# Row softmax on one core: row maximum added, buffers in one ring in place, per-row division, fixed program order, no guard instructions

## The chip, the core and the metric

The kernel runs on one core of one Trainium2 chip. The metric is device time in microseconds, the median of several executions. The span in a profile is about 2 us shorter than that time (161.6 us against 163.6 us before), because it covers the instructions of the program alone.

## The reference

```python
def setup_inputs():
    batch, seq, dim = 16, 1024, 512
    return {"x": np.random.randn(batch, seq, dim).astype(np.float32)}

def reference(x):
    x_max = np.max(x, axis=-1, keepdims=True)
    exp_x = np.exp(x - x_max)
    return (exp_x / np.sum(exp_x, axis=-1, keepdims=True)).astype(np.float32)
```

There are 16384 rows of 512 fp32 numbers: 33.55 MB in and 33.55 MB out.

## The kernel before

The rows are taken in 16 chunks of 128 partitions x 8 rows x 512, 2 MB each. A load goes out from the SP queue. ScalarE (ACT) makes eight exponentials per chunk, one for each row of a partition, and sums them on the way. VectorE (DVE) makes reciprocals of the eight sums and multiplies the whole chunk once by a broadcast. The store goes out from the ACT queue. The row maximum is switched off by an option: these inputs do not overflow without it. POOL's copies and memsets ("guard") compute nothing that is used.

```python
    x_pool = ctx.enter_context(tc.tile_pool(name="xp", bufs=XBUFS))      # 7
    e_pool = ctx.enter_context(tc.tile_pool(name="ep", bufs=EBUFS))      # 4
    ...
    use_max = os.environ.get("SM_USEMAX", "0") == "1"
    ...
    for t in range(nchunks):
        x_tile = x_pool.tile([P, R, d], mybir.dt.float32)
        nc.sync.dma_start(out=x_tile, in_=x_t[t])
        nc.gpsimd.tensor_copy(out=guard_tile, in_=x_tile[:, 0, 0:1])
        if use_max:
            ...  # reduce_max of the chunk to neg_max [P, R]
        e_tile = e_pool.tile([P, R, d], mybir.dt.float32)
        ...
        for r in range(R):
            nc.scalar.activation(
                out=e_tile[:, r, :], in_=x_tile[:, r, :],
                func=mybir.ActivationFunctionType.Exp,
                bias=neg_max[:, r : r + 1] if use_max else 0.0,
                scale=1.0, accum_out=sums[:, r : r + 1],
            )
        ...
        nc.vector.reciprocal(out=recip, in_=sums)
        recip_b = recip.unsqueeze(2).to_broadcast([P, R, d])
        nc.vector.tensor_mul(out=e_tile, in0=e_tile, in1=recip_b)
        nc.scalar.dma_start(out=out_t[t], in_=e_tile)
    for b in range(min(EBUFS, nchunks)):
        e_tile = e_tiles[nchunks - 1 - b]
        nc.gpsimd.memset(e_tile[:, 0, 0:1], 0.0)
```

Here a scheduler chooses the order of instructions on each engine. It gives ACT sixteen exponentials and then two stores, for most pairs of chunks.

The softmax here doesn't subtract the row's maximum and nothing guards it: scores larger than these inputs give would overflow.

## Time and profile before

| | before |
|---|---|
| time | 163.57 us (163.49 to 163.68, 3 runs) |
| span in the profile | 161.6 us |
| DVE / ACT busy | 74.0 us (46%) / 80.8 us (50%) |
| moved by DMA | 67.13 MB, 33.55 read and 33.55 written |

From the page of the kernel before: the span, each engine's busy time, and the row of 40 equal slices. A digit is the busy share of a slice in tenths; the last row is what the DMA engines moved in each slice.

```profile
span 161.6 us, 456 instructions
DVE 74.0 (46%) x32; ACT 80.8 (50%) x257; POOL 18.5 (11%) x24
DVE  0006970994196419082000008941992499069600
ACT  3089519924893481900000199339906970995000
DMA  5999999999999999999999999999999999999993
GB/s 150 434 434 426 434 373 422 432 430 430 438 426 426 446 422 426 450 422 426 446 410 442 438 418 438 434 422 440 426 430 442 418 434 442 418 434 442 418 434 146
```

The DMA row reads 9 from the second slice to the last but one, at about 430 GB/s, while DVE and ACT both have slices of 0. 67.13 MB at 430 GB/s are 156 us (worked out). The start and the end make up the rest. The Trainium skill, "Perfetto Trace Analysis", section What "DMA-bound" means, lists the 16 DMA engines themselves as one thing that such a kernel can be bound on. That is the case here: the DMA row stays at 9 where DVE and ACT fall to 0. What inside the engines or behind them sets the 430 GB/s, the trace does not show.

From the page's groups: line, engine, operation, shapes, count, then total busy us and mean ns of one, then the idle time before it and what ended it.

```profile
L61 ACT ACTIVATE e_tile<-x_tile 128x512 f32<-128x512 f32 x128 | 78.5, 615 | 66.1 <-DMA x_tile<-in_x_dram 35.1
L74 DVE TENSOR_TENSOR e_tile<-e_tile,recip 128x4096 f32<-128x4096 f32 x16 | 70.8, 4425 | 0.5
L49 POOL COPY guard_tile<-x_tile 128x1 f32<-128x1 f32 x16 | 17.9, 1116 | 119.0 <-DMA x_tile<-in_x_dram 119.0
```

From the page, the chain of waits by engine, as shares of the span:

```profile
DMA 52%; ACT 28%; DVE 17%; issue 1%; ACTq 1%; POOLq 0%; SPq 0%
```

The end of the same chain in order of time: start us, length us, what.

```profile
152.35 8.28 DMA out_dram<-e_tile
160.62 0.02 issue
160.65 0.04 POOLq L80
...
160.75 0.11 POOLq L106
```

The last store is issued at 152.35 us and has landed at 160.62 us. The last four stores land 4.8 us apart (POOL's four memsets, which wait for them, start at 146.22, 151.07, 155.92 and 160.75 us), and that is the time of one 2 MB transfer at the full rate. So the DMA engines never ran dry, even with a last store as late as this. The chain names ACT with 28%, but the DMA row is full during those stretches, so ACT time was not paid for there.

### The profile page before, as it was taken

What the parts mean: (1) busy time and instruction counts of PE and PEld (TensorE: products, weight loads), DVE (VectorE), ACT (ScalarE), POOL (GpSimd) and SP (SyncE); (2) the same over time, 40 slices, a digit from 0 to 9 for tenths busy, and PEclk for the clock granted to TensorE, in tenths of its full rate; (3) what the DMA queues carried; (4) which work ended last, traced back from release to release, by engine and by line L of the source; (5) the groups of instructions that cost most, each with busy time, mean ns of one, the idle gap of its engine ahead of it and who ended that gap; (6) DMA issues with size and microseconds to landing.
All of it is one profiled execution on the core that took longest, in us unless ns stands there. A gap on an engine that the chain in (4) does not pass through costs nothing.

```text
span 161.6 us, 456 instructions
## 1 busy us (share of the span) xinstructions
DVE 74.0 (46%) x32; ACT 80.8 (50%) x257; POOL 18.5 (11%) x24
## 2 busy tenths in 40 slices
DVE  0006970994196419082000008941992499069600
ACT  3089519924893481900000199339906970995000
POOL 0000000034090001000000006200082000000000
DMA  5999999999999999999999999999999999999993
GB/s 150 434 434 426 434 373 422 432 430 430 438 426 426 446 422 426 450 422 426 446 410 442 438 418 438 434 422 440 426 430 442 418 434 442 418 434 442 418 434 146
DMA packets 4610, 67.13 MB, mean 415 GB/s; under 512 B 512, under 2 KB 512, under 8 KB 512
## 3 DMA queue, kind: packets, MB, share of 16 engines
q1 hardware_dynamic: 2304, 33.56, 49.4%
q10 hardware_dynamic: 2304, 33.56, 48.5%
q14 instruction: 2, 0.02, 0.0%
HBM read 33.55 MB, written 33.55 MB: 415 GB/s over the span
## 4 chain that ended last, share of the span: by engine, by line
DMA 52%; ACT 28%; DVE 17%; issue 1%; ACTq 1%; POOLq 0%; SPq 0%
DMA x_tile<-in_x_dram 35%; ACT e_tile L61 28%; DMA out_dram<-e_tile 17%; DVE e_tile L74 16%; DVE recip L71 1%; ACTq L76 1%; POOLq L106 0%; POOLq L80 0%; SPq L47 0%
## 5 line engine op out<-in xcount | busy, mean ns | idle before, releaser
L61 ACT ACTIVATE e_tile<-x_tile 128x512 f32<-128x512 f32 x128 | 78.5, 615 | 66.1 <-DMA x_tile<-in_x_dram 35.1
L74 DVE TENSOR_TENSOR e_tile<-e_tile,recip 128x4096 f32<-128x4096 f32 x16 | 70.8, 4425 | 0.5
L71 DVE RECIPROCAL recip<-sums 128x8 f32<-128x8 f32 x16 | 3.2, 203 | 77.7 <-ACT e_tile L61 77.7
L49 POOL COPY guard_tile<-x_tile 128x1 f32<-128x1 f32 x16 | 17.9, 1116 | 119.0 <-DMA x_tile<-in_x_dram 119.0
L61 ACT ACTIVATION_READ_ACCUMULATOR e_tile<-x_tile 128x1 f32 x128 | 23.9, 187 | 0.0
L80 POOL MEMSET e_tile<- 128x1 f32 x4 | 0.4, 99 | 23.1 <-DMA out_dram<-e_tile 23.1
L61 ACT ACT_TABLE_LOAD x1 | 1.3, 1283 | 0.7 <-PEq L95 0.7
L95 POOL MEMSET const-float32-0.0<- 128x1 f32 x1 | 0.1, 99 | 0.2 <-issue 0.2
L95 POOL MEMSET const-uint8-127<- 128x1 uint8 x1 | 0.1, 103 | 0.0
L95 POOL MEMSET const-bfloat16-1.0<- 128x1 bf16 x1 | 0.1, 102 | 0.0
L95 POOL MEMSET const-float32-1.0<- 128x1 f32 x1 | 0.1, 99 | 0.0
## 6 DMA issues: line engine op xcount, KB each, us to landing
x_tile<-in_x_dram SPq DMA_DIRECT2D x16, 2048.0 KB, 42.2
out_dram<-e_tile ACTq DMA_DIRECT2D x16, 2048.0 KB, 18.2
```

The costliest lines, as they stand in the source:

```text
L49: nc.gpsimd.tensor_copy(out=guard_tile, in_=x_tile[:, 0, 0:1])
L61: nc.scalar.activation(out=e_tile[:, r, :], in_=x_tile[:, r, :], func=mybir.ActivationFunctionType.Exp, bias=neg_max[:, r : r + 1] if use_ ...
L71: nc.vector.reciprocal(out=recip, in_=sums)
L74: nc.vector.tensor_mul(out=e_tile, in0=e_tile, in1=recip_b)
L76: nc.scalar.dma_start(out=out_t[t], in_=e_tile)
L80: nc.gpsimd.memset(e_tile[:, 0, 0:1], 0.0)
L95: nc = _bacc.Bacc("TRN2", target_bir_lowering=False, num_devices=1)
```

## The change

The intent is a softmax that is safe for any input (the row maximum is subtracted), without losing time. DVE must read every chunk once more. In exchange, the broadcast multiply becomes eight multiplies by a per-row scalar, everything is done in place in one ring of 12 buffers (a ring is a set of buffers that are used in turn), the order is written down by hand, and the guard instructions go. The core of the diff (imports, view set-up and unchanged arguments cut):

```diff
-    x_pool = ctx.enter_context(tc.tile_pool(name="xp", bufs=XBUFS))
-    e_pool = ctx.enter_context(tc.tile_pool(name="ep", bufs=EBUFS))
-    guard_pool = ctx.enter_context(tc.tile_pool(name="guard", bufs=1))
+SLOTS = {8: 12}
+    data = ctx.enter_context(tc.tile_pool(name="data", bufs=1))
+    def load(k):
+        tiles[k] = data.tile([P, R, d], F32, name=f"x{R}", tag=f"x{R}", bufs=SLOTS[R])
+        nc.sync.dma_start(out=tiles[k], in_=src[k])
-        nc.gpsimd.tensor_copy(out=guard_tile, in_=x_tile[:, 0, 0:1])
+    def rowmax(k):
+        nc.vector.reduce_max(out=shift[k], in_=tiles[k], axis=AX, negate=True)
 ...
-                out=e_tile[:, r, :],
-                in_=x_tile[:, r, :],
-                bias=neg_max[:, r : r + 1] if use_max else 0.0,
+                out=tiles[k][:, r, :],
+                in_=tiles[k][:, r, :],
+                bias=shift[k][:, r : r + 1],
 ...
-        recip_b = recip.unsqueeze(2).to_broadcast([P, R, d])
-        nc.vector.tensor_mul(out=e_tile, in0=e_tile, in1=recip_b)
+        for r in range(R):
+            nc.vector.tensor_scalar_mul(
+                out=tiles[k][:, r, :], in0=tiles[k][:, r, :], scalar1=recip[:, r : r + 1]
+            )
-    for b in range(min(EBUFS, nchunks)):
-        nc.gpsimd.memset(e_tiles[nchunks - 1 - b][:, 0, 0:1], 0.0)
+    with tc.manual_schedule():
+        for k in range(K):
+            load(k); rowmax(k); exps(k)
+            if k >= 1:
+                scale(k - 1); store(k - 1)
+        scale(K - 1); store(K - 1)
```

More of the change, by code (lines that the diff above doesn't have):

```diff
@@ L1 @@
-import os
 from contextlib import ExitStack
@@ L5 @@
 import concourse.tile as tile
-from concourse import bass_utils, mybir
+from concourse import mybir
 from concourse._compat import with_exitstack
+F32 = mybir.dt.float32
+EXP = mybir.ActivationFunctionType.Exp
+AX = mybir.AxisListType.X
+CHUNKS = [8] * 16
+SLOTS = {8: 12}
 @with_exitstack
@@ L22 @@
     n, d = x_flat.shape
-    R = int(os.environ.get("SM_R", "8"))
-    XBUFS = int(os.environ.get("SM_XBUFS", "7"))
-    EBUFS = int(os.environ.get("SM_EBUFS", "4"))
-    rows_per_chunk = P * R
-    assert n % rows_per_chunk == 0
-    nchunks = n // rows_per_chunk
-    x_t = x_flat.rearrange("(t p r) d -> t p r d", p=P, r=R)
-    out_t = out_flat.rearrange("(t p r) d -> t p r d", p=P, r=R)
-    x_pool = ctx.enter_context(tc.tile_pool(name="xp", bufs=XBUFS))
-    e_pool = ctx.enter_context(tc.tile_pool(name="ep", bufs=EBUFS))
@@ L37 @@
-    stats_pool = ctx.enter_context(tc.tile_pool(name="stats", bufs=12))
-    guard_pool = ctx.enter_context(tc.tile_pool(name="guard", bufs=1))
-    use_max = os.environ.get("SM_USEMAX", "0") == "1"
-    guard_tile = guard_pool.tile([P, 1], mybir.dt.float32)
-    e_tiles = []
-    for t in range(nchunks):
-        x_tile = x_pool.tile([P, R, d], mybir.dt.float32)
-        nc.sync.dma_start(out=x_tile, in_=x_t[t])
-        nc.gpsimd.tensor_copy(out=guard_tile, in_=x_tile[:, 0, 0:1])
-        if use_max:
-            neg_max = stats_pool.tile([P, R], mybir.dt.float32)
-            nc.vector.reduce_max(
-                out=neg_max, in_=x_tile, axis=mybir.AxisListType.X, negate=True
-            )
-        e_tile = e_pool.tile([P, R, d], mybir.dt.float32)
-        e_tiles.append(e_tile)
-        sums = stats_pool.tile([P, R], mybir.dt.float32)
+    assert n == P * sum(CHUNKS)
@@ new lines @@
+    src, dst, at = [], [], 0
+    for R in CHUNKS:
+        for flat, views in ((x_flat, src), (out_flat, dst)):
+            part = flat[at : at + P * R, :]
+            views.append(part.rearrange("(p r) d -> p r d", r=R))
+        at += P * R
+    data = ctx.enter_context(tc.tile_pool(name="data", bufs=1))
+    stats = ctx.enter_context(tc.tile_pool(name="stats", bufs=4))
+    K = len(CHUNKS)
+    tiles = [None] * K
+    shift = [None] * K
+    sums = [None] * K
+    def load(k):
+        R = CHUNKS[k]
+        tiles[k] = data.tile([P, R, d], F32, name=f"x{R}", tag=f"x{R}", bufs=SLOTS[R])
+        nc.sync.dma_start(out=tiles[k], in_=src[k])
@@ L60, with exps @@
+    def rowmax(k):
+        R = CHUNKS[k]
+        shift[k] = stats.tile([P, R], F32, name=f"shift{R}", tag=f"shift{R}")
+        nc.vector.reduce_max(out=shift[k], in_=tiles[k], axis=AX, negate=True)
+    def exps(k):
+        R = CHUNKS[k]
+        sums[k] = stats.tile([P, R], F32, name=f"sums{R}", tag=f"sums{R}")
         for r in range(R):
             nc.scalar.activation(
-                out=e_tile[:, r, :],
-                in_=x_tile[:, r, :],
-                func=mybir.ActivationFunctionType.Exp,
@@ L65 @@
-                bias=neg_max[:, r : r + 1] if use_max else 0.0,
+                out=tiles[k][:, r, :],
+                in_=tiles[k][:, r, :],
+                func=EXP,
+                bias=shift[k][:, r : r + 1],
                 scale=1.0,
-                accum_out=sums[:, r : r + 1],
+                accum_out=sums[k][:, r : r + 1],
             )
-        recip = stats_pool.tile([P, R], mybir.dt.float32)
-        nc.vector.reciprocal(out=recip, in_=sums)
-        recip_b = recip.unsqueeze(2).to_broadcast([P, R, d])
@@ L74, with scale @@
-        nc.vector.tensor_mul(out=e_tile, in0=e_tile, in1=recip_b)
-        nc.scalar.dma_start(out=out_t[t], in_=e_tile)
-    for b in range(min(EBUFS, nchunks)):
-        e_tile = e_tiles[nchunks - 1 - b]
-        nc.gpsimd.memset(e_tile[:, 0, 0:1], 0.0)
+    def scale(k):
+        R = CHUNKS[k]
+        recip = stats.tile([P, R], F32, name=f"recip{R}", tag=f"recip{R}")
+        nc.vector.reciprocal(out=recip, in_=sums[k])
+        for r in range(R):
+            nc.vector.tensor_scalar_mul(
+                out=tiles[k][:, r, :],
+                in0=tiles[k][:, r, :],
+                scalar1=recip[:, r : r + 1],
+            )
@@ L84, with store @@
+    def store(k):
+        nc.scalar.dma_start(out=dst[k], in_=tiles[k])
+    with tc.manual_schedule():
+        for k in range(K):
+            load(k)
+            rowmax(k)
+            exps(k)
+            if k >= 1:
+                scale(k - 1)
+                store(k - 1)
+        scale(K - 1)
+        store(K - 1)
 _INS = ['x']
```

## The prediction

> **What bounds the kernel now.** The DMA engines. The page's 40-slice row shows DMA at 9 in every slice but the first and last, at about 430 GB/s, while VectorE (DVE) is busy 46% and ScalarE (ACT) 50%. Of the 161.6 us span, 67.13 MB at about 430 GB/s are 156 us; the rest is the start (full rate only from about 4 us, windows of 1 us) and the end (last landing at 160.6 us). One 2 MB transfer costs 4.85 us of the engines (the last stores land 4.8 us apart); 32 of them are the kernel. Where loads and stores are both queued, each queue gets about 2.15 MB per 10 us, half each (queue table by windows of 10 us). The chain of waits names ACT 28% and DVE 17%, but under them the DMA row stays full: a backlog hides them.
>
> **What changes.**
> - DVE gains a row maximum per chunk, 128x4096 to 128x8. The existing 128x4096 multiply takes 4.43 us; the maximum should take the same. The Trainium skill, "VectorE: DVE Perf Modes" (perf-mode tier table), gives tensor_reduce one element per cycle and fp32 tensor_scalar two, tensor_tensor one. 16 x 4.43 = +71 us.
> - The multiply becomes 128 instructions of 128x512. From the trace: 4.43 us is about 4.27 us of elements plus 0.16 us fixed. At the double rate one takes 0.27 us plus up to 0.16 us: 0.33 to 0.43 us, an estimate; 8 are 2.7 to 3.4 us instead of 4.43. That is -16 to -28 us.
> - DVE in all: 74 us to about 116-130 us, 7.4-8.0 us a chunk, against 9.7 us of DMA a chunk (load plus store).
> - ACT: the same 128 exponentials at 0.61 us (bias from a tile). POOL's 16 guard copies (17.9 us) and the final memset go; about 0.2 us of that was on the critical path, at the end.
> - Bytes are unchanged. Buffers go from 7+4 to 12 shared.
>
> **On the critical path.** Almost nothing. The first store is issued near 23.5 us (before: 23.2); loads keep the engines full until then. Afterwards both queues share evenly, so the last load should land near 133 us (before: about 137). Then maximum, exponentials and scaling take about 14 us, which gives the last store at about 147 us. At that time three stores are still queued (before issued its last at 152.35 us and lost nothing). So DVE has a margin: by my bookkeeping of these durations, queueing starts to cost only when one chunk's DVE work exceeds about 8.3 us.
>
> **Prediction: 163.3 us, 162.3 to 166.0 with 80%.** Faster by over 2%: 2%. Within 2%: 86%. Slower by over 2%: 12%.
>
> **What would show each step right.** DMA at 9 in all middle slices and 430 GB/s; span 160.5-162; DVE 116-132 us busy (72-82%), with the maximum at 4.4 us and tensor_scalar at 0.33-0.43 us; ACT about 80 us; the last store issued near 147 us, before the DMA queue runs dry; first store near 23-24 us.
>
> **What would make it wrong.** If tensor_scalar does not get the double rate (about 0.6 us each), a chunk costs 9.4 us on DVE; then the last store is issued near 164 us and the time is about 172 us. If the maximum is slower than 4.6 us or tensor_scalar nears 0.5 us, holes appear in the DMA row after about 140 us, costing 1-4 us. ACT's in-order store issue could also be held by DMA semaphores shared with loads. A gain could only come from a higher DMA rate or from the dip to 373 GB/s at 20-24 us going away, at most about 1 us.

## The result, and the profile after

| | before | after |
|---|---|---|
| time | 163.62 us (163.49 to 163.79, 4 runs) | 163.14 us (163.01 to 163.32, 4 runs) |
| ratio | | 0.9972 (95%: 0.9958 to 0.9986) |
| span | 161.6 us | 161.3 us |
| DVE / ACT busy | 74.0 / 80.8 us | 123.8 / 93.2 us |
| last store issued | 152.35 us | 149.49 us |

A ratio is the mean time of one kernel's runs over the mean of the other's in the same rounds, so it is not quite the ratio of the medians. Within 2% this counts as the same time; the small gain of 0.3% is nevertheless outside its interval of noise.

From the page of the changed kernel, the same rows:

```profile
span 161.3 us, 527 instructions
DVE 123.8 (77%) x160; ACT 93.2 (58%) x257; POOL 0.2 (0%) x4
DVE  0088799999999999985970079999999999957000
ACT  0037994959596867067002996859595959591000
DMA  6999999999999999999999999999999999999993
GB/s 163 431 427 427 431 435 378 418 445 431 423 439 431 421 435 431 431 439 418 439 435 427 431 427 435 435 425 435 431 427 439 431 427 427 431 435 431 431 435 171
```

DVE has 50 us more work, and the DMA row has not changed. The groups of the changed kernel:

```profile
L63 ACT ACTIVATE x<-x,shift 128x512 f32<-128x512 f32 x128 | 90.5, 709 | 44.1 <-DVE shift L57 21.4
L57 DVE TENSOR_REDUCE shift<-x 128x8 f32<-128x4096 f32 x16 | 70.6, 4415 | 9.7 <-DMA x<-in_x_dram 9.7
L77 DVE TENSOR_SCALAR x<-x,recip 128x512 f32<-128x512 f32 x128 | 52.1, 482 | 0.6
```

The maximum costs what the broadcast multiply cost, 4.41 us. A multiply of 128x512 has a mean of 482 ns, but eight of them take less than eight times that. One chunk on DVE, from the timeline (start us, length us, engine and operation):

```profile
22.28 4.41 DVE L57 TENSOR_REDUCE shift<-x 128x8 f32<-128x4096 f32 x1
26.61 0.20 DVE L75 RECIPROCAL recip<-sums 128x8 f32<-128x8 f32 x1
26.84 3.26 DVE L77 TENSOR_SCALAR x<-x,recip 128x512 f32<-128x512 f32 x8
30.01 4.41 DVE L57 TENSOR_REDUCE shift<-x 128x8 f32<-128x4096 f32 x1
```

Consecutive records overlap: the eight take 3.26 us, so the step from one start to the next is (3.26 - 0.48) / 7 = 0.40 us. A chunk takes 7.73 us of DVE from one maximum to the next, against 9.7 us for its load and store on the DMA engines.

The chain of waits of the changed kernel now names DVE with 31%:

```profile
DMA 52%; DVE 31%; ACT 6%; SPq 2%; issue 1%; ACTq 1%; DVEq 0%
```

A reader who took that line for a cost would expect to gain from a faster DVE. The experiments show otherwise.

One thing in the timeline of ACT looks dangerous, the issue of the stores (start us, length us):

```profile
53.32 0.34 ACTq L84 DMA_DIRECT2D out_dram<-x  x1
...
69.46 0.34 ACTq L84 DMA_DIRECT2D out_dram<-x  x1
...
87.38 0.34 ACTq L84 DMA_DIRECT2D out_dram<-x  x1
87.82 0.72 ACT L63 ACTIVATE x<-x,shift 128x512 f32<-128x512 f32 x1 [12.14 <-DMA x<-in_x_dram]
...
143.52 0.34 ACTq L84 DMA_DIRECT2D out_dram<-x  x1
...
149.49 0.34 ACTq L84 DMA_DIRECT2D out_dram<-x  x1
```

The sixth and seventh stores wait for the landing of the ninth and eleventh load. In the built program, loads and stores take turns with eight DMA semaphores (a semaphore is the counter that tells that a transfer has landed), and these stores take the semaphores of those loads. ACT works in order, so it stands idle for 12.14 us and then DVE does too (the two 0 in its row). The DMA row stays at 9 all the same: while no store is queued, the loads take the full rate (from 84 to 87 us the load queue's packets took 98% of the engines' time). The loads have moved their bytes just after 130 us, and the stores alone fill the rest. The hold leaves DVE with a backlog: from 93.6 us to 140 us it works without a pause, and the last maximum starts at 135.67 us although the last load has landed at 132.6 us.

### The profile page after: what moved, and what is told of

The parts are those of the page before. It is cut to its first block, busy times and chain, and to the rows that moved or that the text cites. A ratio compares the mean times of both kernels' runs of the same rounds, so it can differ in the third digit from the quotient of the medians.

```text
span 161.3 us, 527 instructions
## 1 busy us (share of the span) xinstructions
DVE 123.8 (77%) x160; ACT 93.2 (58%) x257; POOL 0.2 (0%) x4
## 4 chain that ended last, share of the span: by engine, by line
DMA 52%; DVE 31%; ACT 6%; SPq 2%; issue 1%; ACTq 1%; DVEq 0%
DMA x<-in_x_dram 52%; DVE shift L57 16%; DVE x L77 14%; ACT x L63 6%; SPq L52 2%; DVE recip L75 1%; ACTq L84 0%; DVEq L121 0%; ACTq L63 0%
## 5 line engine op out<-in xcount | busy, mean ns | idle before, releaser
L63 ACT ACTIVATE x<-x,shift 128x512 f32<-128x512 f32 x128 | 90.5, 709 | 44.1 <-DVE shift L57 21.4
L57 DVE TENSOR_REDUCE shift<-x 128x8 f32<-128x4096 f32 x16 | 70.6, 4415 | 9.7 <-DMA x<-in_x_dram 9.7
L77 DVE TENSOR_SCALAR x<-x,recip 128x512 f32<-128x512 f32 x128 | 52.1, 482 | 0.6
L63 ACT ACTIVATION_READ_ACCUMULATOR x<-x,shift 128x1 f32 x128 | 24.0, 187 | 0.0
```

Source lines behind the costliest of these rows:

```text
L57: nc.vector.reduce_max(out=shift[k], in_=tiles[k], axis=AX, negate=True)
L63: nc.scalar.activation(out=tiles[k][:, r, :], in_=tiles[k][:, r, :], func=EXP, bias=shift[k][:, r : r + 1], scale=1.0, accum_out=sums[k][: ...
L77: nc.vector.tensor_scalar_mul(out=tiles[k][:, r, :], in0=tiles[k][:, r, :], scalar1=recip[:, r : r + 1],)
```

## The experiments

All kernels ran beside the kernel before on the same chip. All were correct except the one without computing, which is wrong.

| run | time, us | ratio to before (95%) |
|---|---|---|
| changed kernel | 163.14 | 0.9972 (0.9958 to 0.9986) |
| nomax | 162.96 | 0.9969 (0.9953 to 0.9986) |
| dma_only | 162.75 | 0.9951 (0.9937 to 0.9965) |
| extra1 | 163.37 | 0.9989 (0.9974 to 1.0004) |
| wide_mul | 166.61 | 1.0187 (1.0172 to 1.0202) |
| extra3 | 168.54 | 1.0304 (1.0287 to 1.0321) |
| before_noguard | 163.07 | 0.9975 (0.9962 to 0.9989) |
| ring8 | 162.85 | 0.9956 (0.9936 to 0.9976) |
| ring6 | 163.11 | 0.9972 (0.9954 to 0.9991) |
| split_first | 163.03 | 0.9962 (0.9949 to 0.9974) |
| before_max | 179.85 | 1.0996 (1.0981 to 1.1011) |
| before_max_narrow | 178.81 | 1.0931 (1.0915 to 1.0948) |
| two_rings_wide | 164.22 | 1.0037 (1.0022 to 1.0052) |

### nomax: is the maximum free?

```diff
-            rowmax(k)
-                bias=shift[k][:, r : r + 1],
+                bias=0.0,
```

> The changed kernel without the row maximum (bias 0.0), all else as it is; right for these inputs, since their exponentials do not overflow. Theory that the maximum is wholly hidden behind the DMA engines: 163.1 us (162.8 to 163.4), although 70.6 us of DVE work go. Rival, the maximum costs something that another part of the change (ring, guards) gives back: 162 us or less. The exponential of 128x512 took 0.613 us before and 0.707 us in the changed kernel: if the bias read from a tile causes that it is 0.61 us here, if working in place causes it it stays 0.71 us.

It took 162.96 us. 70.6 us of DVE work went away and the ratio moved from 0.9972 to 0.9969: the maximum is hidden. The run also settled the exponential:

```profile
L63 ACT ACTIVATE x<-x 128x512 f32<-128x512 f32 x128 | 78.5, 614 | 61.2 <-DMA x<-in_x_dram 61.2
```

It works in place and takes 614 ns, so working in place costs nothing. The run before_max below writes to another buffer with a bias tile and takes 708 ns. The 94 ns belong to the bias read from a tile. The Trainium skill, "ScalarE: Activation LUTs", section What ACT_TABLE_LOAD costs, states that each [128,1] pointer operand of an ACTIVATE adds about 93 ns; traces agree.

### dma_only: where is the floor?

```diff
             load(k)
-            rowmax(k)
-            exps(k)
             if k >= 1:
-                scale(k - 1)
                 store(k - 1)
-        scale(K - 1)
         store(K - 1)
```

> Loads and stores of the changed kernel with no computing (the output is the input, wrong on purpose): 67.1 MB through the same 16 DMA engines. Theory that the changed kernel sits on the floor of its transfers: 163 us, at most 0.5 us under it (162.5 to 163.3). Rival, the computing stage still costs the DMA engines something (starts, contention for memory): 161 us or less.

It took 162.75 us. The output is the input. With no computing at all, the same 67.1 MB need all but 0.4 us of the changed kernel's time. With the transfers issued in this order, nothing done on DVE or ACT can gain more than that.

### extra1, wide_mul and extra3: how much DVE work is free?

extra1 and extra3 add one and three useless multiplies per chunk; this is the edit for three.

```diff
+        for j in range(3):
+            spare = stats.tile([P, d], F32, name="spare", tag="spare", bufs=1)
+            nc.vector.tensor_scalar_mul(
+                out=spare, in0=tiles[k][:, j, :], scalar1=recip[:, j : j + 1]
+            )
```

> The changed kernel with one useless tensor_scalar of 128x512 more per chunk (0.4 us each, 6.4 us of DVE in all, a chunk of 8.1 us). Margin theory: the last store comes 8 x 0.4 = 3.2 us later, about 152.7 us, inside the margin of about 3.7 us: 163.1 to 163.8 us. Rival, the chain of waits names DVE with 31% and so DVE time is paid for in full or by that share: 165 us (by the share) to 169.5 us (in full).

> Three useless tensor_scalar of 128x512 more per chunk (1.2 us, a chunk of 8.9 us). Margin theory: the last store comes 9.5 us later, 5.8 us beyond the margin: 169 us (166.5 to 171.5), and the DMA row shows holes after about 140 us. Rival, busy share: 163.1 us with DVE at 88%.

wide_mul undoes one part of the change:

```diff
-        for r in range(R):
-            nc.vector.tensor_scalar_mul(
-                out=tiles[k][:, r, :],
-                in0=tiles[k][:, r, :],
-                scalar1=recip[:, r : r + 1],
-            )
+        nc.vector.tensor_mul(
+            out=tiles[k], in0=tiles[k], in1=recip.unsqueeze(2).to_broadcast([P, R, d])
+        )
```

> The changed kernel with the division put back to one broadcast multiply of 128x4096 per chunk (4.43 us) in place of eight of 128x512 (3.26 us together). DVE then needs about 4.33 + 0.2 + 4.4 = 8.9 us a chunk, 144 us in all, about 86-90% of the span. Margin theory (a chunk of DVE work is free up to about 8.3 us, because the last store then still comes before the store queue runs dry; the margin at the last store is about 3.7 us, and each of the last 8 chunks is delayed by 1.15 us): about +5.5 us, 168.5 us (166 to 171). Rival, the busy share decides (an engine under 100% busy costs nothing): 163.1 us.

The measured times were 163.37, 168.54 and 166.61 us. The last store is the thing to follow. The DMA row of extra1, and the issue of its last store in the timeline:

```profile
DMA  5999999999999999999999999999999999999994
```

```profile
153.31 0.34 ACTq L89 DMA_DIRECT2D out_dram<-x  x1
```

The same of wide_mul:

```profile
DMA  6999999999999999999999999999999999993976
```

```profile
157.58 0.34 ACTq L81 DMA_DIRECT2D out_dram<-x  x1
```

And of extra3, with its rate by slices:

```profile
DMA  5999999999999999999999999999999999790975
GB/s 161 428 428 432 432 432 385 425 428 434 421 440 427 432 428 432 436 421 436 428 432 428 428 436 425 442 425 432 425 432 432 429 440 425 336 440 4 440 314 252
```

```profile
159.62 0.34 ACTq L89 DMA_DIRECT2D out_dram<-x  x1
```

| | DVE per chunk, us | last store issued, us | later than in the changed kernel, us | span, us | longer, us | difference of the two |
|---|---|---|---|---|---|---|
| changed kernel | 7.73 | 149.49 | | 161.3 | | |
| extra1 | 8.25 | 153.31 | 3.82 | 161.3 | 0.0 | |
| wide_mul | 8.90 | 157.58 | 8.09 | 164.7 | 3.4 | 4.7 |
| extra3 | 9.17 | 159.62 | 10.13 | 166.7 | 5.4 | 4.7 |

DVE per chunk is the distance of two store issues near 130 us. Two runs give the same margin of 4.7 us, and so does a third reading: the last store takes 11.0 us from issue to landing in the changed kernel, behind others, and 6.3 us in wide_mul and extra3, where it runs alone. From there on every microsecond of delay is paid in full. Up to 3.8 us of delay costs nothing (extra1, and ring6 below with a last store at 153.25 us and a span of 161.2 us). Between 3.8 and 8.1 us the corner is extrapolated, and it is not sharp: two_rings_wide below has its last store 4.5 us later (153.95 us) and a span 0.7 us longer.

Each microsecond added to a chunk moves the last store by about 7 us (3.82 / 0.52, 8.09 / 1.17, 10.13 / 1.44), so the margin is used up at about 7.73 + 4.7 / 7 = 8.4 us per chunk. It is 7 and not 15 because the seventh store is issued between 87.4 and 87.6 us in all four kernels, when the eleventh load lands; DVE time added before that is absorbed. The 8.4 us therefore belong to this ring and this order of semaphores: two_rings_wide needs 8.90 us a chunk, as wide_mul does, and loses 2.4 us less.

The rivals fall. DVE was busy 86% in wide_mul (142.3 of 164.7 us) and it cost 1.9%, so "below 100% busy is free" is wrong; two_rings_wide has the same DVE work at 88% and cost 0.4%. In extra1 DVE work grew by 7.5 us at no cost to the span, so "the share in the chain is paid for" is wrong too (its median is 0.2 us above the changed kernel's, within the intervals; the share would have been 2 us). The recorded figure for wide_mul was 168.5 us, 1.9 us too high: the margin had been put at 3.7 us, and the delay of the last store at 9.2 us (8 x 1.15) where 8.09 was measured.

This also shows what the cut multiply was for. With the maximum and the broadcast multiply together the time would have gone up by 1.9% in this ring, not down (by 0.4% with two rings, as two_rings_wide shows below).

### before_noguard: where do the 0.3% come from?

```diff
-        nc.gpsimd.tensor_copy(out=guard_tile, in_=x_tile[:, 0, 0:1])
 ...
-    for b in range(min(EBUFS, nchunks)):
-        e_tile = e_tiles[nchunks - 1 - b]
-        nc.gpsimd.memset(e_tile[:, 0, 0:1], 0.0)
```

> The kernel before without its 16 guard copies and 4 final memsets on POOL, all else unchanged. The changed kernel was 0.3% (0.45 us) faster than the kernel before; theory: about 0.2 us of that is the final memset and what follows it after the last landing (the time from the last landing to the end of the span was 1.0 us before and 0.8 us after). Expected 163.3 us, a ratio of 0.998 to 0.9995. Rival, the guards held loads back and cost more: 162.5 us or less. Rival, nothing: ratio 1.000.

It took 163.07 us, ratio 0.9975, somewhat more than expected (a ratio of 0.998 or above). Taking the guards out of the kernel before gives the same time as the whole change: 0.9975 and 0.9972 cannot be told apart. Part of it is the memset after the last landing that the chain of before ends with. How the rest is made up is open; it is about 0.2 us, too little for one profile.

### ring8 and ring6: does the depth matter?

```diff
-SLOTS = {8: 12}
+SLOTS = {8: 8}     # ring8; 6 in ring6
```

> The changed kernel with a ring of 8 buffers in place of 12. Theory: the DMA engines stay fed as long as a load can be issued while stores queue; bookkeeping of the durations gives no loss down to 6 buffers: 163.1 us. Rival, the ring of 12 is what hides the row maximum: 165 us or more.

> The changed kernel with a ring of 6 buffers, half the memory. Bookkeeping: no loss or the beginning of one, 163.1 to 165 us (with 5 it would be about 3.8 us more). Rival, depth matters in proportion: 168 us or more.

They took 162.85 and 163.11 us. The ring of 12 gains nothing over half of it. In ring6 no store waits for a later load's landing (ACT's waits name no such load) and the time is the same, so the 12 us for which ACT stands idle in the changed kernel cost nothing.

### split_first: can the start be shortened?

```diff
-        nc.sync.dma_start(out=tiles[k], in_=src[k])
+        eng = nc.scalar if k == 1 else nc.sync
+        eng.dma_start(out=tiles[k], in_=src[k])
```

> The changed kernel with its second load issued from the ACT queue, so that two queues start at once. In the windows of 1 us the first 3 us of transfers move 213, 115 and 311 GB/s instead of 430: about 1.5 us are lost. If one queue's start limits this, up to 1 us less: 162.2 us. If the engines' or the memory's first answers limit it whatever the queue: 163.1 us.

It took 163.03 us. The interval holds the changed kernel's ratio, and in the trace the same three windows move 164, 197 and 262 GB/s, together no more than before. A second queue does not shorten the start.

### before_max, before_max_narrow and two_rings_wide: what does the fixed order do?

before_max is the kernel before with its own option switched on (`SM_USEMAX` 1 instead of 0).

> The kernel before with only the row maximum switched on (its own option), so with two rings, broadcast multiply, scheduler's order and guards. DVE 74 + 71 = 145 us; 9.0 us a chunk. Margin theory: slower, 168 to 174 us, since the maximum is only affordable with the cheaper multiply; the order that the scheduler chose lets maxima run ahead, which may save some of it. Rival, the maximum is free whatever stands beside it as DVE stays under 90% busy: 163.6 us. The exponential here writes to another buffer than it reads: 0.71 us means that the bias tile makes it longer, 0.61 us that working in place does.

It took 179.85 us, more than the expected 168 to 174. From the timeline of DVE in before_max:

```profile
80.56 17.39 DVE L53 TENSOR_REDUCE neg_max<-x_tile 128x8 f32<-128x4096 f32 x4
```

The scheduler put four maxima in a row, and during these 17.39 us no multiply was done, so no store could be issued. The group of the exponential settles the question from nomax:

```profile
L61 ACT ACTIVATE e_tile<-x_tile,neg_max 128x512 f32<-128x512 f32 x128 | 90.5, 708 | 63.3 <-DVE e_tile L74 48.9
```

Two runs then divided the suspects. before_max_narrow keeps scheduler, rings and guards and cuts the multiply:

```diff
-        recip_b = recip.unsqueeze(2).to_broadcast([P, R, d])
-        nc.vector.tensor_mul(out=e_tile, in0=e_tile, in1=recip_b)
+        for r in range(R):
+            nc.vector.tensor_scalar_mul(
+                out=e_tile[:, r, :], in0=e_tile[:, r, :], scalar1=recip[:, r : r + 1]
+            )
```

> The kernel before with its row maximum switched on and the multiply cut into eight tensor_scalar of 128x512, in the scheduler's order, with two rings and guards: DVE 7.7 us a chunk as in the changed kernel. Here the scheduler puts at most two maxima in a row, but leaves six chunks at the end without one. Theory: mostly hidden again, 163.4 to 166 us; the six last chunks are paced by ACT (6 us each), so a small loss is possible. Rival, the scheduler's order is bad whatever the multiply costs: 172 us or more.

two_rings_wide starts from wide_mul and goes back to two rings:

```diff
-SLOTS = {8: 12}
+SLOTS = {8: 7}
+    epool = ctx.enter_context(tc.tile_pool(name="ep", bufs=4))
+        outs[k] = epool.tile([P, R, d], F32, name="e", tag="e")
-                out=tiles[k][:, r, :],
+                out=outs[k][:, r, :],
-            out=tiles[k], in0=tiles[k], in1=recip.unsqueeze(2).to_broadcast([P, R, d])
+            out=outs[k], in0=outs[k], in1=recip.unsqueeze(2).to_broadcast([P, R, d])
-        nc.scalar.dma_start(out=dst[k], in_=tiles[k])
+        nc.scalar.dma_start(out=dst[k], in_=outs[k])
```

> Row maximum and broadcast multiply of 128x4096 in the changed kernel's fixed program order, but with the two rings of before (7 for the input, 4 for the exponentials, not in place) and no guards. It stands between the run wide_mul (one ring, 166.61 us) and the run before_max (two rings, scheduler's order, guards, 179.85 us). Theory that the order alone made before_max slow (four maxima in a row on DVE at 80 to 98 us, in which no store could be issued, and five chunks at the end paced by ACT at 5.98 us each): 166.6 us, at most 168. Rival, the two rings cost it: 175 us or more.

They took 178.81 and 164.22 us. My expectation for before_max_narrow (163.4 to 166 us) was wrong and its rival right: in the scheduler's order the cheaper multiply saves 1 us of 16. two_rings_wide (166.6 us expected) rules out that the two rings alone cost it. The waits of ACT tell what the scheduler's order does (engine and line waited for: us in total, times, longest). In before_max_narrow:

```profile
ACT e_tile L61 <- DVE e_tile L74: 59.2, 15, 10.9
...
ACT e_tile L61 <- DVE neg_max L53: 4.8, 2, 3.1
```

In the changed kernel:

```profile
ACT x L63 <- DVE shift L57: 21.4, 10, 3.1
ACT x L63 <- DMA x<-in_x_dram: 18.6, 2, 12.1
```

In the scheduler's order (read from the built program) ACT comes to most stores in the middle of a chunk's exponentials, and stands there until DVE has multiplied the chunk before, 59.2 us in all. The changed kernel has no wait of that kind: the store of a chunk comes after all exponentials of the next, and DVE has multiplied by then. In before_max_narrow the last six stores are 6.17 us apart in the timeline (138.82 to 169.67 us in five steps), slower than the 4.85 us of DMA that one takes, and the DMA row has holes:

```profile
DMA  5999999999999999999999779999937879768975
```

two_rings_wide ran faster than wide_mul by 2.4 us, which was not expected. Its DMA row is nearly full:

```profile
DMA  6999999999999999999999999999999999999984
```

In wide_mul the deep ring lets loads run ahead, and a store was held for a load's landing as shown above; DVE then lost 3.7 us:

```profile
ACT x L63 <- DMA x<-in_x_dram: 9.9, 1, 9.9
...
DVE recip L75 <- ACT x L63: 5.9, 3, 3.7
```

In two_rings_wide that wait is smaller:

```profile
DVE recip L78 <- ACT e L66: 2.2, 2, 1.2
```

Its last store is issued at 153.95 us, 3.6 us before that of wide_mul. That the shared semaphores are the cause is read from the two traces and not tested by a run of its own. before_max and before_max_narrow differ from the fixed-order kernels in their guards as well. Guards cost 0.25% in before_noguard, and the traces of the two runs speak against them: the load queue (SP) waits 80 and 83 us for ACT's exponentials to free input buffers, and no load waits for a guard copy. No run with the scheduler's order and without guards was made together with the maximum.

## Why the prediction was right

- **The bound.** The DMA engines were the bound before and are the bound after. The DMA row and dma_only show it: 162.75 us without any computing.
- **The time.** 163.3 us was predicted and 163.14 us measured, in the range and in the class with 86%.
- **The DVE sum.** 116 to 130 us predicted, 123.8 measured; a chunk of 7.4 to 8.0 us predicted, 7.73 measured; the maximum at 4.41 us. The Trainium skill's tier table ("VectorE: DVE Perf Modes", perf-mode tier table) gives fp32 tensor_scalar twice the rate of tensor_tensor. The step of 0.40 us for 512 elements is below the 0.53 us that one element per cycle would need at the page's 0.96 GHz (an estimate).
- **A detail off inside that sum.** One tensor_scalar was to take 0.33 to 0.43 us. Its record is 0.48 us long; only the step from one to the next, 0.40 us, is in the range. The estimate for eight (2.7 to 3.4 us) holds at 3.26 us because records overlap. Half of 4.43 / 8 us is 0.28 us; the measured step has 0.12 us on top.
- **ACT was mis-sized.** "About 80 us" was predicted and 93.2 us measured, since the bias tile adds 94 ns to each of 128 exponentials (12 us). The skill's page had the figure and I did not look there. ACT was not the bound, so nothing came of it.
- **The margin.** The prediction put the limit at 8.3 us of DVE per chunk. The runs give about 8.4 us. The mechanism is right: stores still queued behind the last one hide DVE. That the figure came so close may be partly luck, for its parts, as the prediction and the expectations give them, were off: three stores queued near 147 us (the trace has two that have not landed), a margin of 3.7 us (4.7), and 8 us of delay for each microsecond of a chunk (7).
- **The timeline.** First store at 22.4 us (predicted 23.5). The last load landed at 132.6 us (predicted 133), though the queues did not share evenly all the way. The last store came 13.8 us after the last maximum began (predicted 14). DVE began that maximum 3 us after the landing, because of its backlog, so the last store was issued at 149.5 us and not at 147.
- **The held stores.** The prediction named stores held by shared DMA semaphores as a way to be wrong. They were held, ACT stood idle up to 12 us, and it cost nothing here; in wide_mul it seems to have cost about 2 us, which is not tested.
- **The small gain.** 0.2 us for the end was about half of the guards' 0.4 us. The rest of the change gives no time at all that these runs can show.
- **What the prediction did not see.** It treated the order as given. In the scheduler's order, with its rings and guards, the maximum cost 15 to 16 us, whichever multiply was used. The prediction could hold because the order was read from the built program, with one maximum between two chunks' multiplies.

## What to carry to other kernels

When the DMA row is full from end to end, ask of added work when the last store will be issued, and whether the store queue is still full at that moment. Neither the busy share nor the share in the chain of waits answers this; moving the last store on purpose does, and here it gave about 4.7 us twice, with a loss of 0.7 us already at 4.5 in a third run. Here the program order was worth more than the cost of an instruction: cutting the multiply saved 1 us in the scheduler's order and 3.5 us in the fixed one with one ring, and the fixed order, together with what went with it, saved about 15.6 us with either multiply.

## What the Trainium skill lacked or had wrong

- "DMA: Bandwidth & Descriptors", section Bandwidth, says that for HBM to SBUF transfers the HBM side (about 358 GB/s) binds. For a lone core that is wrong here: one core moved about 430 GB/s for over 150 us, half reads and half writes. The 425 GB/s that the same section measured for a large single-core transfer fits. "Perfetto Trace Analysis", section Engine Utilization, has it right: it says that a core that is active alone can pull more than its 358 GB/s share, up to about 435 GB/s.
- No page that was read says what follows when loads and stores take turns with few DMA semaphores: ACT stood idle for 12.14 us behind a store that waited for an unrelated load's landing.
- No page that was read says how far an engine that is not the bound may grow before it costs. Here the answer was a margin of about 4.7 us at the last store, with a loss of 1.9% at 86% busy in one kernel and of 0.4% at 88% in another.
